# Merge gates of two branches projected earlier, inside the gated mixer and the attention mixer, and kept in HBM until their merges

## The chip, the cores and the metric

The kernel runs on one NeuronCore of a Trainium2 chip, as one launch. The metric is the device time of the launch in microseconds. Before the change it is 2548.67 us, the median of three runs that lie between 2547.56 and 2550.62 us. The profile is that of one further execution.

The engines are named as in the profile: PE (TensorE, the matrix engine), DVE (VectorE), ACT (ScalarE), POOL (GpSimd) and SP (SyncE, which here only issues DMAs). PEld is PE's loading of stationary operands.

## What is computed

Two layers of a hybrid backbone work on 640 tokens (512 latent tokens of one request, 128 context tokens of another) with a model width of 1024. Within a layer one input projection feeds three parallel mixers and three merge gates. The part that matters here, cut from the reference:

```python
(a_q, a_k, a_v, a_g, b_q, b_k, b_v, b_r, c_q, c_k, c_v,
 m_a, m_b, m_c) = jnp.split(h @ P['w_in'][l], points, axis=-1)
...  # y_a: retention of A; y_b: gated linear attention of B; y_c: differential attention of C
wb = P['w_branch'][l]
merged = (jax.nn.sigmoid(m_a) * (y_a.astype(dt) @ wb[0])
          + jax.nn.sigmoid(m_b) * (y_b.astype(dt) @ wb[1])
          + jax.nn.sigmoid(m_c) * (y_c.astype(dt) @ wb[2]))
out = merged @ P['w_out'][l]
```

The gates m_a, m_b and m_c, each 1024 wide, depend on the layer's input h alone, not on the mixers. The mixers' outputs are 512 wide. After the output projection follow a residual with LayerNorm, a gated MLP with a short convolution, and a second LayerNorm.

## The kernel before, in words

Activations lie transposed: a tile is 128 channels by 640 tokens, a "row" of SBUF. There are 59 rows (L486, L499), given out and taken back as tiles live and die; the last seven free ones are given only in program order. The layer's input h is 16 rows: eight tiles of 128 channels, each split into a high and a low fp32r part (hh, hl). Weights are split in the same way, and every product is made of three matmuls: high by high, low by high and high by low.

Weights come as blocks of 128 x 1024 in one fixed order, BLOCKS (L123). For each block a DMA on SP's queue loads w, ACT copies it to whi, and DVE or POOL forms wlo (`weights`, L731). Each of the three stages has three buffers, used strictly in that order. `take` (L756) fetches the next block and asserts that it is the one wanted, so the order of the blocks and the order of the program are one. `take` also paces the modulation: after every second block taken, the dot products of one further column of the modulation map are put into the program (`ada`, L686: two loads, four dot products on DVE). Blocks in the set QUIET (L124), which holds all blocks ahead of mixer A's, do not count for this pace.

`project` (L877) makes 128 output channels for all tokens: 48 matmuls into one of two PSUM tiles of the pool behind `slot`. A second pool of two, `mslot`, serves mostly the inner products of the mixers. A merge product (`gemm` into pbr) is 24 matmuls, since the mixers' outputs are 512 wide; one weight block holds two of them.

The order of the work is not that of the text. All operations are put into a list (`Program.add`, L225), and a planner (`place`, L291) builds a static order for every engine with modelled costs: for each engine in turn it takes the ready operation that stands first in the program, if its tile can have a buffer. Operations are offered up to 120 us of PE work ahead of where PE is, loads up to 40 us (L133). The hardware then runs these fixed orders, each engine and SP's queue in order, held by semaphores.

A layer runs in this order of the program:

- `mix_b` (L1003), the gated mixer, for two head pairs t = 0, 1: projections q, k, v and gate r; then a loop of nine levels (chunk lengths m = 1 to 256, counted by `lev`), each of which makes decayed queries and keys (eq, ek), a few small matmuls (psl, psp) and masked copies into st and stp; then the product with the values (po) and a normalization.
- `mix_a` (L1192), the retention mixer.
- `mix_c` (L1280), the attention mixer, as a generator with one step per head, with the merges of the second and the first branch put between its steps: four merges of branch 1 (mixer B) after heads 0 and 1, four of branch 0 (mixer A) after heads 2 and 3.
- the merges of branch 2 (mixer C), then the output projection (pout), the first LayerNorm, the MLP (pfa, pfb, pdn) and the second LayerNorm.

One merge is a pass of the loop in `branch` (L1437): it projects the gate's 128 channels (pmm, of block M_A, M_B or M_C), takes the tanh on ACT into a row g, makes the product pbr of the mixer's output with the branch's weights, multiplies on DVE ((g + 1) * pbr, in place), and adds to merged[j] on POOL, unless it is the first branch to be merged.

Of the kernel before, what the change touches and what calls it, by code (L numbers as in the profile page):

```python
# [10 lines left out]
F32 = mybir.dt.float32  # L11
F32R = mybir.dt.float32r
I32 = mybir.dt.int32
AF = mybir.ActivationFunctionType
# [59 lines left out]
def _blocks():  # L74
    b = []
    for t in range(2):
        b += [("in", B_Q + 128 * t), ("in", B_K + 128 * t)]
        b += [("v", B_V + 256 * t, i) for i in range(2)] if t else [("vg", i) for i in range(3)]
        b += [("in", B_R + 256 * t), ("in", B_R + 256 * t + 128)]
    for t in range(2):  # L80
        b += [("in", A_Q + 128 * t), ("in", A_K + 128 * t), ("v", A_V + 256 * t, 0), ("v", A_V + 256 * t, 1),
              ("in", A_G + 256 * t), ("in", A_G + 256 * t + 128)]
    for h in range(4):
        if h % 2 == 0:
            b += [("v", C_V + 128 * h, 0), ("v", C_V + 128 * h, 1)]
        b += [("in", C_Q + 128 * h), ("in", C_K + 128 * h)]
    return b
# [15 lines left out]
def _blocks_branch(x, m):  # L103
    b = []
    for j in range(8):
        b.append(("in", m + 128 * j))
        if j % 2 == 0:
            b.append(("br", x, j))
    return b


def _order():

    a = _blocks()
    c0 = a.index(("v", C_V, 0))
    o, c = a[:c0], a[c0:]
    fb, fa = _blocks_branch(1, M_B), _blocks_branch(0, M_A)
    o += c[0:4]
    o += c[4:6] + fb[0:6] + c[6:10] + fb[6:12] + c[10:12] + fa[0:6] + fa[6:12]
    return o + _blocks_branch(2, M_C) + _blocks_tail()  # L120


BLOCKS = _order()  # L123
# [360 lines left out]
def hybrid_kernel(ctx, tc, io):  # L484
# [392 lines left out]
    def project(ws, hs, name, *want, pool=slot):  # L877
        w = take(ws, *want)
        ps = pool(name)
        gemm(ps, w, 0, 8, hs)  # L880
        return ps
# [118 lines left out]
        return r[:, 0:512].rearrange("p (h x) -> p h x", h=4)  # L1000


    def mix_b(l, ws, hs, ys, save):  # L1003
        def mask(i, n=4):
            m, o = (m0, 128 * i) if i < 5 else (m1, 128 * (i - 5))
# [28 lines left out]
        for t in range(2):  # L1034
# [61 lines left out]
            while m < TL:  # L1096
                n = T if m < 128 else TL

                def v(x):
                    return x[:, 0:n].rearrange("p (b u m) -> p b u m", u=2, m=m)  # L1100

                eq = row("eq")
                act(v(eq)[:, :, 1, :], v(F)[:, :, 1, :], AF.Exp, scale=0.0625)
                act(v(eq)[:, :, 0, :], v(R)[:, :, 0, :], AF.Exp, scale=0.0625)
                tt(eq[:, 0:n], eq[:, 0:n], q[:, 0:n], MUL)
                if m == 1:
                    ek = k
                else:
                    ek = row("ek")
                    act(v(ek)[:, :, 0, :], v(G)[:, :, 0, :], AF.Exp, scale=0.0625)  # L1110
                    act(v(ek)[:, :, 1, :], v(H)[:, :, 1, :], AF.Exp, scale=0.0625)
                    tt(ek[:, 0:n], ek[:, 0:n], k[:, 0:n], MUL)
                bc = [128, n // (2 * m), m]
                tt(v(G)[:, :, 0, :], v(G)[:, :, 0, :], v(F)[:, :, 1, m - 1:m].to_broadcast(bc), ADD, POOL)
                tt(v(H)[:, :, 1, :], v(H)[:, :, 1, :], v(R)[:, :, 0, 0:1].to_broadcast(bc), ADD, POOL)
                tt(v(F)[:, :, 1, :], v(F)[:, :, 1, :], v(F)[:, :, 0, m - 1:m].to_broadcast(bc), ADD, POOL)
                tt(v(R)[:, :, 0, :], v(R)[:, :, 0, :], v(R)[:, :, 1, 0:1].to_broadcast(bc), ADD, POOL)
                if m < 256:
                    ps = mslot("psl")
                    for s in range(4):  # L1120
                        c = slice(128 * s, 128 * s + 128)
                        d = c if m < 128 else slice(128 * (s ^ 1), 128 * (s ^ 1) + 128)
                        mm_pair(*((bank(ps, h)[:, c], ek[a, c], eq[a, d]) for h, a in enumerate(rows)))
                    for h in range(2):
                        if m < 128:
                            copy_pred(out=chunks(st[h][:, 0:TL]), mask=mask(lev).bitcast(I32), data=chunks(bank(ps, h)))
                        else:
                            act(p128[h][:, 0:TL], bank(ps, h))
                else:
                    kk = [row("kk", F32R) for _ in range(2)]  # L1130
                    stack(kk, slice(0, TL), ek[:, 0:TL])
                    qq, ql = twice(eq, "q", TL)
                    for i in range(2):
                        ps = mslot("psl")
                        d = slice(256 * (1 - i), 256 * (1 - i) + 256)
                        for j in range(2):
                            c = slice(128 * (2 * i + j), 128 * (2 * i + j) + 128)
                            out = [bank(ps, h)[:, 256 * j:256 * j + 256] for h in range(2)]
                            mm_pair(*((out[h], kk[h][:, c], qq[h][:, d]) for h in range(2)), stop=False)
                            mm_pair(*((out[h], kk[h][a, c], ql[a, d]) for h, a in enumerate(rows)), start=False)  # L1140
                        for h in range(2):
                            act(p256[h][i][:, 0:512], bank(ps, h))
                if m < 128:
                    held.append((ek, eq, lev))
                    if len(held) == 2:
                        prompts()
                if m == 64:
                    for e, x in ((0, G), (1, H)):
                        kd = row("kd")
                        act(kd[:, 0:128], x[:, TL:T], AF.Exp, scale=0.0625)  # L1150
                        tt(kd[:, 0:128], kd[:, 0:128], k[:, TL:T], MUL)
                        states(kd[:, 0:128], vs, io["sgla"][l, e, t])
                lev += 1
                m *= 2
            qd = []
# [273 lines left out]
    for l in range(L):  # L1429
# [7 lines left out]
        def branch(x, mo, y):  # L1437
            yy = []
            for k in range(4):
                yh, yl = row("yh", F32R), row("yl", F32R)  # L1440
                split(yh, yl, y[k])
                yy.append((yh, yl))
            wb = None
            for j in range(8):
                ps = project(ws, hs, "pmm", "in", mo + 128 * j)
                g = row("g")
                act(g, ps[:, P0:P0 + T], AF.Tanh, scale=0.5)
                if j % 2 == 0:
                    wb = take(ws, "br", x, j)
                pb = slot("pbr")  # L1450
                gemm(pb, wb, 512 * (j % 2), 4, yy)
                stt(g, g, 1.0, pb[:, P0:P0 + T], ADD, MUL)
                if len(merged) < 8:
                    merged.append(g)
                else:
                    tt(merged[j], merged[j], g, ADD, POOL)
                yield
# [269 lines left out]
```

## Time and profile before

| | |
|---|---|
| median of three runs | 2548.67 us (2547.56 to 2550.62) |
| profiled execution | 2548.93 us |
| its span, from the first to the last instruction | 2547.2 us |
| mean granted PE clock | 0.985 |
| PE busy | 2467.7 us, 97% |
| DVE busy | 1619.7 us, 64% |
| ACT busy | 1117.3 us, 44% |
| POOL busy | 514.5 us, 20% |
| DMA, mean over the span | 95 GB/s, 242.87 MB |

A row of the table of stretches holds a stretch of the span in us, its length, and the busy time of each engine within it; "PEclk" is the share of full speed that PE's clock was granted. In a group or a timeline row, "out<-in" are the names that the program gave the tiles, L is the line of a helper, and what follows "<-" behind an idle time is what ended it. Nearly all matmuls are issued by two helpers (L533, L542), so they are told apart by the tile that they write: pmm are merge gates, pbr merge products, psl and psp the level products of the gated mixer, pvv value projections, psc scores of attention.

In this execution layer 0's gated mixer ends near 225 us, its attention mixer runs from about 342 to 640, its third branch to 731, and its output projection to 795. In layer 1 the gated mixer's level loops lie in 1352 to 1478, the attention mixer in 1597 to 1896, and the third branch ends at 1986.

### The profile page before, as it was taken

What the parts mean: (1) busy time and instruction counts of PE and PEld (TensorE: products, weight loads), DVE (VectorE), ACT (ScalarE), POOL (GpSimd) and SP (SyncE); (2) the same over time, 40 slices, a digit from 0 to 9 for tenths busy, and PEclk for the clock granted to TensorE, in tenths of its full rate; (3) what the DMA queues carried; (4) which work ended last, traced back from release to release, by engine and by line L of the source; (5) the groups of instructions that cost most, each with busy time, mean ns of one, the idle gap of its engine ahead of it and who ended that gap; (6) DMA issues with size and microseconds to landing.
All of it is one profiled execution on the core that took longest, in us unless ns stands there. A gap on an engine that the chain in (4) does not pass through costs nothing.

```text
span 2547.2 us, 41288 instructions
## 1 busy us (share of the span) xinstructions
PE 2467.7 (97%) x16762; PEld 2349.6 (92%) x16762; DVE 1619.7 (64%) x2898; ACT 1117.3 (44%) x1813; POOL 514.5 (20%) x391
## 2 busy tenths in 40 slices
PE   7999999999999999999989899999999999999997
PEld 4888889999998999999978789999999989999997
DVE  5788886566678865656868877744553564334346
ACT  3687654444325322223457676543442253122234
POOL 0452220121232600000346501100211132000001
PEclk9999999999999999999989899999999999999999
DMA  7122222322442333333422132112113222222222
GB/s 272 59 94 90 88 71 92 107 82 97 150 151 92 132 108 116 103 122 122 137 92 69 57 106 71 61 52 76 60 59 116 93 79 77 75 76 67 84 69 93
DMA packets 90335, 242.87 MB, mean 95 GB/s; under 512 B 10145, under 2 KB 16673, under 8 KB 90017
## 3 DMA queue, kind: packets, MB, share of 16 engines
q1 hardware_dynamic: 90144, 240.23, 28.5%
q8 instruction: 132, 2.16, 0.4%
q14 instruction: 59, 0.48, 0.1%
HBM read 232.85 MB, written 7.34 MB: 94 GB/s over the span
## 4 chain that ended last, share of the span: by engine, by line
PE 87%; DVE 6%; ACT 4%; DMA 2%; issue 1%; POOL 0%; SPq 0%; ACTq 0%; DVEq 0%; POOLq 0%
PE pmm L533 13%; PE pfb L533 12%; PE pfa L533 12%; PE pdn L533 12%; PE pbr L533 7%; PE pvv L533 6%; PE pout L533 4%; PE pcq L533 2%; PE pck L533 2%; PE pag L533 2%; PE psc L542 2%; PE ptc L533 1%; PE pr L533 1%; PE po L533 1%; PE psl L542 1%; DVE hf L580 1%
## 5 line engine op out<-in xcount | busy, mean ns | idle before, releaser
L554 ACT ACTIVATE whi<-w 128x1024 fp32r<-128x1024 f32 (+1 forms) x318 | 331.1, 1041 | 853.0 <-PE pdn L533 217.2
L566 DVE TENSOR_TENSOR wlo<-w,whi 128x1024 fp32r<-128x1024 f32 (+2 forms) x273 | 346.0, 1269 | 336.3 <-ACT whi L554 328.9
L566 POOL TENSOR_TENSOR wlo<-w,whi 128x1024 fp32r<-128x1024 f32 (+2 forms) x45 | 107.2, 2384 | 1221.9 <-ACT whi L554 1034.2
L533 PE MATMUL pmm<-hh,wlo 128*128 128x384 f32 (+1 forms) x768 | 239.2, 311 | 0.0
L533 PE MATMUL pmm<-hl,whi 128*128 128x384 f32 (+1 forms) x768 | 239.1, 311 | 0.0
L533 PE MATMUL pmm<-hh,whi 128*128 128x384 f32 (+1 forms) x768 | 238.7, 311 | 0.0
L533 PE MATMUL pfa<-hl,whi 128*128 128x384 f32 (+1 forms) x704 | 218.8, 312 | 4.5 <-DVE hl L580 4.3
L533 PE MATMUL pfa<-hh,whi 128*128 128x384 f32 (+1 forms) x704 | 218.8, 311 | 3.4 <-ACT hh L554 2.8
L533 PE MATMUL pfb<-hl,whi 128*128 128x384 f32 (+1 forms) x704 | 218.6, 311 | 0.0
L533 PE MATMUL pfb<-hh,whi 128*128 128x384 f32 (+1 forms) x704 | 218.5, 310 | 0.0
L533 PE MATMUL pdn<-fh,whi 128*128 128x384 f32 (+1 forms) x704 | 218.1, 310 | 0.0
L533 PE MATMUL pfb<-hh,wlo 128*128 128x256 f32 (+1 forms) x704 | 218.1, 310 | 0.0
L533 PE MATMUL pfa<-hh,wlo 128*128 128x384 f32 (+1 forms) x704 | 217.9, 310 | 0.0
L533 PE MATMUL pdn<-fl,whi 128*128 128x384 f32 (+1 forms) x704 | 217.9, 310 | 0.0
L533 PE MATMUL pdn<-fh,wlo 128*128 128x384 f32 (+1 forms) x704 | 217.7, 309 | 0.0
L533 PEld LDWEIGHTS pmm<-hh,whi 128*128 128x128 f32 x768 | 144.5, 188 | 1.0 <-issue 0.6
L533 PEld LDWEIGHTS pmm<-hl,whi 128*128 128x128 f32 x768 | 144.4, 188 | 0.9 <-issue 0.8
L533 PEld LDWEIGHTS pmm<-hh,wlo 128*128 128x128 f32 x768 | 144.5, 188 | 0.7 <-issue 0.5
L533 PE MATMUL pvv<-whi,hh 128*128 128x256 f32 (+1 forms) x480 | 138.7, 289 | 2.1 <-ACT q L554 1.0
L533 PE MATMUL pvv<-wlo,hh 128*128 128x256 f32 (+1 forms) x480 | 136.4, 286 | 3.8 <-DVE wlo L566 3.0
L533 PEld LDWEIGHTS pfa<-hl,whi 128*128 128x128 f32 x704 | 132.5, 188 | 7.5 <-DVE hl L580 7.4
L533 PE MATMUL pvv<-whi,hl 128*128 128x256 f32 (+1 forms) x480 | 137.5, 287 | 0.7 <-ACT z L554 0.7
(393 smaller groups left out, 6834.3 us busy)
## 6 DMA issues: line engine op xcount, KB each, us to landing
w<-W SPq DMA_DIRECT2D x270, 512.0 KB, 3.5
wada<-adaT SPq DMA_DIRECT2D x160, 256.0 KB, 3.8
w<-W SPq DMA_DIRECT2D x42, 448.0 KB, 3.2
wada<-adaW SPq DMA_DIRECT2D x32, 256.0 KB, 5.4
x<-xT SPq DMA_DIRECT2D x8, 320.0 KB, 6.1
dist<-rc SPq DMA_DIRECT2D x8, 320.0 KB, 3.6
xa<-xT SPq DMA_DIRECT2D x8, 320.0 KB, 6.3
xsave<-xa SPq DMA_DIRECT2D x8, 320.0 KB, 5.1
```

Of the source, the lines that this page charges most:

```text
L533: prog.add(("PE",), lambda e: nc.tensor.matmul(real(out), real(lhsT), real(rhs), start=start, stop=stop), [out], [lhsT, rhs], {"PE": c})
L542: nc.tensor.matmul(real(o), real(w), real(r), start=start, stop=stop)
L554: prog.add(("ACT",), lambda e: nc.scalar.activation(out=real(out), in_=real(in_), func=func, **{k: real(x) for k, x in kw.items()}), [out] ...
L566: prog.add(eng, lambda e: ENG[e].tensor_tensor(out=real(out), in0=real(a), in1=real(b), op=op), [out], [a, b], vcost(out.n), late=late, po ...
L580: prog.add(eng, lambda e: ENG[e].scalar_tensor_tensor(out=real(out), in0=real(a), scalar=real(s), in1=real(b), op0=op0, op1=op1), [out], [ ...
```

## The change

The gates of branch 1 (M_B) are no longer projected in its merges but in the gated mixer: a new helper `early` projects the 128 channels, takes the tanh into a row and stores the row to a tensor of its own in HBM. It is called behind the levels with an odd `lev` (1, 3, 5, 7), so four gates fall to each head pair. The gates of branch 2 (M_C) are projected by the same helper inside the passes of branch 1, that is, between the heads of the attention mixer, where M_B stood. In a pass of `branch` whose gate was kept, the row g is loaded from HBM and neither projection nor tanh is made. Branch 0 is as before. The order of the weight blocks follows. As the M_B blocks now stand ahead of mixer A's, they belong to QUIET and do not count for the pace of the modulation columns.

```diff
@@ _blocks
         b += [("in", B_R + 256 * t), ("in", B_R + 256 * t + 128)]
+        b += [("in", M_B + 128 * j) for j in range(4 * t, 4 * t + 4)]
@@ _blocks_branch
     for j in range(8):
-        b.append(("in", m + 128 * j))
+        if m is not None:
+            b.append(("in", m + 128 * j))
         if j % 2 == 0:
             b.append(("br", x, j))
@@ _order
-    fb, fa = _blocks_branch(1, M_B), _blocks_branch(0, M_A)
+    fb, fa = _blocks_branch(1, M_C), _blocks_branch(0, M_A)
     o += c[0:4]
     o += c[4:6] + fb[0:6] + c[6:10] + fb[6:12] + c[10:12] + fa[0:6] + fa[6:12]
-    return o + _blocks_branch(2, M_C) + _blocks_tail()
+    return o + _blocks_branch(2, None) + _blocks_tail()
@@ hybrid_kernel
+    def early(l, ws, hs, x, j):
+
+        ps = project(ws, hs, "pmm", "in", (M_A, M_B, M_C)[x] + 128 * j)
+        g = row("g")
+        act(g, ps[:, P0:P0 + T], AF.Tanh, scale=0.5)
+        name = f"gate{l}{x}{j}"
+        kept[l, x, j] = V(Tile_(None, [128, T], F32, name, dram.tile([128, T], F32, name=name)))
+        dma(kept[l, x, j], g, load=False)
+
+    kept = {}
+
@@ mix_b, in the level loop
+                if lev % 2:
+                    early(l, ws, hs, 1, 4 * t + lev // 2)
                 lev += 1
                 m *= 2
@@ branch
             for j in range(8):
-                ps = project(ws, hs, "pmm", "in", mo + 128 * j)
+                if x == 1:
+                    early(l, ws, hs, 2, j)
                 g = row("g")
-                act(g, ps[:, P0:P0 + T], AF.Tanh, scale=0.5)
+                if (l, x, j) in kept:
+                    dma(g, kept[l, x, j])
+                else:
+                    ps = project(ws, hs, "pmm", "in", mo + 128 * j)
+                    act(g, ps[:, P0:P0 + T], AF.Tanh, scale=0.5)
```

## The prediction

> **What bounds the kernel now.** I read the shares of the engines first, then the chain that ended last.
>
> ```profile
> PE 2467.7 (97%) x16762; PEld 2349.6 (92%) x16762; DVE 1619.7 (64%) x2898; ACT 1117.3 (44%) x1813; POOL 514.5 (20%) x391
> ...
> PE 87%; DVE 6%; ACT 4%; DMA 2%; issue 1%; POOL 0%; SPq 0%; ACTq 0%; DVEq 0%; POOLq 0%
> ```
>
> TensorE is busy for 97% of the span and carries 87% of the chain. The edit neither adds nor removes a matmul, so it can gain only where PE is idle or runs at a lower clock, and lose only where it opens a new gap. The second view is a table of stretches, cut at the stages (columns: stretch, length, busy time of PE, its weight loads, DVE, ACT, POOL, then clock, DMA share, GB/s). The gated mixer's level loops lie in 96:130 and 171:225 (layer 0, head pair 0 and 1) and in 1352:1395 and 1428:1478 (layer 1). 342:640 is layer 0's attention mixer with the merges woven in, 640:731 its third branch, 731:795 its output projection, and 1896:1986 is layer 1's third branch.
>
> ```profile
> 96.00:130.00 34.00, 30.34 (x283) 27.31 (x282) 31.12 (x39) 19.05 (x36) 24.26 (x25) 1.00 0.05 17
> 130.00:171.00 41.00, 40.56 (x289) 36.80 (x288) 32.33 (x37) 34.84 (x66) 19.92 (x19) 1.00 0.36 120
> 171.00:225.00 54.00, 48.07 (x363) 41.03 (x362) 48.17 (x74) 33.92 (x73) 26.21 (x26) 0.91 0.17 52
> ...
> 1352.00:1395.00 43.00, 40.80 (x367) 37.22 (x364) 35.06 (x46) 31.51 (x63) 26.18 (x30) 1.00 0.09 29
> ...
> 1428.00:1478.00 50.00, 39.47 (x297) 33.44 (x296) 45.19 (x72) 28.73 (x61) 22.60 (x24) 0.76 0.18 52
> ...
> 342.00:640.00 298.00, 295.06 (x2022) 280.81 (x2021) 203.30 (x398) 141.71 (x248) 51.87 (x32) 1.00 0.28 92
> 640.00:731.00 91.00, 91.00 (x623) 91.00 (x623) 60.75 (x120) 24.93 (x30) 31.76 (x16) 1.00 0.41 139
> 731.00:795.00 64.00, 62.69 (x413) 61.10 (x412) 53.83 (x103) 24.86 (x36) 20.23 (x10) 1.00 0.45 148
> ...
> 1896.00:1986.00 90.00, 90.00 (x619) 90.00 (x618) 29.27 (x31) 24.43 (x30) 16.70 (x8) 1.00 0.29 100
> ```
>
> PE idles 54.00 - 48.07 = 5.93 us and 50.00 - 39.47 = 10.53 us in the level loops of head pair 1, and 3.66 and 2.20 us in those of head pair 0. The first difference is that head pair 0 had the projections of head pair 1 to fill in, and head pair 1 little. In those two loops DVE is at 89% and 90%: their chain of level steps is DVE's. The third branch, from which PE work is taken, has no idle time at all. The timeline of PE and four stretches at the halved clock show the rest:
>
> ```profile
> 1437.22 3.08 PE L542 MATMUL psl<-eq,ek 64*128 64x128 f32 x32 [2.99 <-DVE st L601]
> ...
> 1442.47 2.08 PE L542 MATMUL psl<-eq,ek 64*128 64x128 f32 x16
> ...
> 1446.07 1.16 PE L542 MATMUL psl<-eq,ek 64*128 64x128 f32 x16 [0.81 <-DVE st L601]
> ```
>
> ```profile
> 202.41:212.65 10.24, 9.73 (x50) 8.83 (x47) 10.03 (x13) 8.04 (x18) 6.01 (x6) 0.50 0.36 117
> ...
> 1438.00:1444.90 6.90, 5.95 (x54) 5.41 (x52) 6.67 (x10) 3.85 (x10) 6.90 (x8) 0.51 0.14 38
> 1444.90:1448.30 3.40, 1.52 (x22) 1.17 (x20) 3.37 (x6) 1.11 (x3) 3.40 (x6) 1.00 0.27 82
> 1448.30:1465.30 17.00, 12.88 (x78) 11.01 (x79) 15.22 (x27) 6.96 (x16) 3.60 (x4) 0.50 0.07 14
> ```
>
> At the halved clock sixteen psl matmuls take 2.08 us instead of 1.16: 0.92 of 2.08, or 44% of the time, is lost.
>
> **The change part by part.** *Gates of the second branch into the level loops.* A projection is 48 matmuls, a merge product 24:
>
> ```profile
> 1901.64 7.08 PE pmm L533 x48
> ...
> 1929.80 3.55 PE pbr L533 x24
> ...
> L554 ACT ACTIVATE g<-pmm x48: 682/687/707, 388.7 to 1983.6; 128x640 f32<-128x640 f32 x48
> ```
>
> Each head pair gets four gates, 4 x 7.08 = 28.3 us of PE work that depends on nothing but weights. The PE's own level work leaves 10.5 us idle at most per loop, so the filler is enough. It stands after an odd level in program order and ahead of the next one; the planner takes the lowest ready operation, single matmuls at a time, so the gate goes first and the level step waits a few us, while PE stays busy. What stays idle is what the plan misjudged; I take for head pair 1 the idle time that its neighbour with filler has: 3.66 in layer 0, 2.20 in layer 1. Gain 5.93 - 3.66 = 2.3 and 10.53 - 2.20 = 8.3, together **10.6 us**. Bounds: 0 (the gates run after the loops) and all four, 22.3 us.
>
> *The clock.* With PE busy the halving goes. Busy time in the halved stretches is 9.73 + 5.95 + 12.88 = 28.6 us, of which 44% is saved: **12.6 us**; bounds 0 and half, 14.3. The row 1444.90:1448.30, PE busy 1.52 of 3.40 us and halved right behind it, says that a thin stretch is enough to lower the clock; 130:171, full, kept 1.00. [...]
>
> *What moves with them.* Eight weight blocks per layer (load, ACT, DVE or POOL split) and eight tanh (0.687 us each) move into the gated mixer: DVE gets 8 x 1.31 = 10.5 us more there, per layer. That lies under 8 x 7.08 = 56.6 us of new PE work, so DVE's share falls; without that cover it would cost its 10.5 us. The weights in layer 0's and 1's gated mixer drive no modulation columns (they are in QUIET), so four columns of layer 0 come later, in stages with DVE at 64% on the mean: nothing.
>
> *Gates of the third branch into the attention mixer.* In 342:640 the second branch's merges keep their PE work: 7.08 us of the third's gate in place of 7.08 us of their own. Nothing is gained, PE has 2.9 us idle there. At its end the third branch used to give 56.6 us more PE work per layer; is that cover missed? In layer 1:
>
> ```profile
> 1896.17 0.83 DVE L566 TENSOR_TENSOR yl<-rstd,yh 128x640 fp32r<-128x640 f32 x1 [0.81 <-ACT yh L554]
> ```
>
> The last attention output is split at 1897.0, and PE works on products of the first branch until the third's first gate begins at 1901.64. The third's own product, which now stands there, is ready 4.6 us before. So the cover is enough, with that margin; the loss is bounded by 0 and, if the last head came 10 us later, 5.4 us. I take **1 us** for layer 1, near to the row.
>
> *Gate tiles through HBM.* Per layer 16 stores and 16 loads of 320 KB. The nearest rows are the residual's, stored and loaded again, beside a weight block's:
>
> ```profile
> w<-W SPq DMA_DIRECT2D x270, 512.0 KB, 3.5
> ...
> xsave<-xa SPq DMA_DIRECT2D x8, 320.0 KB, 5.1
> xa<-xsave SPq DMA_DIRECT2D x8, 320.0 KB, 6.1
> ```
>
> A load lands 6.1 us after issue, and its store (5.1 us) was issued a stage earlier, so only the row of SBUF can hold it back. Loads may be issued 40 us of PE work ahead, and the 16 rows of the input's split halves come free after the first branch's last gate, which is earlier than before. Taken as nothing; bound: the first load has to wait for those rows, 6.1 us less the 3.5 us of the first product, 2.6 us per layer, within the 5.4 above. A store waits on SP's queue for its tanh, and the next weight loads stand behind it; see the rivals.
>
> *The third branch, now short.* It becomes 8 x 3.55 = 28.4 us instead of 85.0. In layer 1 DVE's 29.27 us (less eight weight splits, 10.5) fit. In layer 0 the modulation columns and the scaling of the residual run there too. Here are the costliest groups of DVE, then of POOL, in 640:795:
>
> ```profile
> L566 DVE TENSOR_TENSOR wlo<-w,whi 128x1024 fp32r<-128x1024 f32 x22 | 28.8, 1312 | 14.1 <-ACT whi L554 13.6
> L586 DVE SCALAR_TENSOR_TENSOR wada<-wada,sB 128x512 f32<-128x512 f32 x27 | 21.7, 813 | 0.2
> L586 DVE SCALAR_TENSOR_TENSOR junk<-wada,sB 128x512 f32<-128x512 f32 x27 | 20.1, 755 | 3.1 <-DMA wada<-adaT 3.1
> ...
> L566 DVE TENSOR_TENSOR ml<-g,mh 128x640 fp32r<-128x640 f32 x8 | 6.6, 825 | 9.5 <-ACT mh L554 9.5
> ...
> L566 DVE TENSOR_TENSOR acc<-acc,xa 128x384 f32<-128x384 f32 (+1 forms) x8 | 4.5, 561 | 0.2
> ...
> L580 DVE SCALAR_TENSOR_TENSOR hf<-xa,ms,rs 128x256 f32<-128x256 f32 (+1 forms) x4 | 3.5, 940 | 1.2 <-ACT rs L554 1.2
> ...
> L566 DVE TENSOR_TENSOR xa<-xa,mu 128x256 f32<-128x256 f32 x8 | 3.2, 471 | 0.3 <-ACT mu L554 0.3
> ```
>
> ```profile
> L566 POOL TENSOR_TENSOR g<-g 128x640 f32<-128x640 f32 x9 | 18.6, 2070 | 60.9 <-DVE g L580 60.9
> L572 POOL TENSOR_SCALAR xa<-xa 128x640 f32<-128x640 f32 x8 | 15.9, 2002 | 1.3 <-DMA xa<-xT 1.3
> L566 POOL TENSOR_TENSOR wlo<-w,whi 128x1024 fp32r<-128x1024 f32 x4 | 10.1, 2514 | 39.3 <-ACT whi L554 39.3
> L566 POOL TENSOR_TENSOR sq<-sq 128x384 f32<-128x384 f32 x5 | 7.7, 1534 | 2.8 <-DVE sq L566 2.6
> ```
>
> The stretch of 155 us becomes 155 - 56.6 = 98.4 us. DVE's 60.75 + 53.83 = 114.6 us lose eight splits (10.5) and four columns: 27 pairs of dot products are 13.5 columns at (21.7 + 20.1) / 13.5 = 3.1 us, so 12.4. There stay 91.7 us, 93% of the stretch. It fits, but in the first 28 us a merge may wait for a column's dot products. On PE that costs between 0 and, when DVE and POOL can't overlap, 19.4 us (rival 1). I take **5 us**: nearer to 0, since DVE alone still fits.
>
> *Sum:* -10.6 - 12.6 + 1 + 5 = -17.2 us. The profiled execution took 2548.93 us, of which its span is 2547.2; it is 0.26 us above the median of 2548.67, so on the median **2531.5 us**.
>
> **The rivals.** *1: VectorE and GpSimd take turns in layer 0's third branch.* All the DVE groups shown take their data from SBUF: 28.8 + 21.7 + 20.1 + 6.6 + 4.5 + 3.5 + 3.2 = 88.4 us, and POOL's 52.3. Less the 10.5 and the 12.4 there are 117.8 us for 98.4, 19.4 too many. With that in the place of 5 the time is 2548.67 - 10.6 - 12.6 + 1 + 19.4 = 2545.9, too near to no change to be told from it. For it: the adds g<-g take 2.07 us on the mean in layer 0 here, after 1.56 at the least elsewhere:
>
> ```profile
> L566 POOL TENSOR_TENSOR g<-g x32: 1555/1688/2651, 554.2 to 1987.3; 128x640 f32<-128x640 f32 x32
> ```
>
> Against it: columns may run 40 us ahead, where DVE is at 68%. [...]
>
> *2: the gates do not fill.* If the two PSUM slots that the gates need are held by other tiles through the level loops, the gates run behind them. The first two terms are 0 and the losses stay: 2548.67 + 6 = 2554.7. For it: in 1428:1478 projections of the next mixer stood ready and PE idled. Against it: a gate's slot is freed by one tanh of 0.687 us, not by a queue of DVE work.
>
> *3, slower: SP's queue.* SP issues in order, and each of the 32 stores waits for its tanh; weight loads behind it are late.
>
> ```profile
> SPq L618 <- ACT kt L554: 119.1, 16, 35.9
> ...
> PE pvv L533 <- DVE wlo L566: 3.0, 2, 2.0
> ...
> L554 ACT ACTIVATE whi<-w 128x1024 fp32r<-128x1024 f32 (+1 forms) x318 | 331.1, 1041 | 853.0 <-PE pdn L533 217.2
> ```
>
> For it: the 16 small stores of states made SP wait 119.1 us, 35.9 at once. Against it: PE waited for split weights 3.0 us in all, since three blocks stand ready, 21 us of PE work. It decides once a store is waited for longer than that. A block then costs 3.5 (landing) + 1.04 (ACT) + 1.31 (DVE) = 5.8 us of idle PE; at one store in four, 8 x 5.8 = 46 us, and the time is 2531.5 + 46 = 2578.
>
> *4: everything is recovered:* 22.3 + 14.3 us and no loss, 2512.
>
> **How the numbers follow.** The forecast has 0.62, its own range 2520 to 2544. Rival 1 at its full price has 0.14, rival 2 0.07, rival 3 0.09, rival 4 0.08. A measurement of this kernel can tell 0.2%, 5.1 us, from no change. Faster: 0.62 + 0.08 = 0.70; same: rival 1, 0.14; slower: 0.07 + 0.09 = 0.16. The range 2515 to 2549 reaches from the greater part of rival 4 to rival 1 and leaves out rivals 2 and 3.
>
> **What would show it.** Right: gate projections (pmm) between the psl of all four level loops; the halved clock gone around 202 to 213 and 1438 to 1465; PE idle of head pair 1's loops down to about that of head pair 0; the third branch some 28 us long in both layers and the attention mixers as long as before. Wrong: PE idle beside pbr or pout behind DVE or POOL in layer 0 (rival 1), pmm grouped behind the loops (rival 2), PE waiting for weight splits in the mixers with SP behind a gate's tanh (rival 3). The forecast falls if the level loops lose less than 10 us of idle and halved time together.

## The result and the profile after

The changed kernel takes 2524.65 us (median; 2523.45 to 2525.73), beside 2548.11 us for the kernel before on the same chip: a ratio of 0.9908, with a 95% interval of 0.9891 to 0.9925. That is 24.0 us less than the median before the prediction, and 23.5 less than the runs beside it; 17.2 were forecast. The shares of the engines on the page of the changed kernel:

```profile
PE 2458.0 (97%) x16762; PEld 2338.9 (93%) x16762; DVE 1613.0 (64%) x2898; ACT 1114.4 (44%) x1813; POOL 513.5 (20%) x387
```

The matmuls are the same 16762. PE's busy time fell by 9.7 us all the same, since a matmul at the halved clock is busy for longer (2.08 against 1.16 us for sixteen psl in the kernel before). The level loops of the changed kernel, in the table of stretches (stretch, length, busy time of PE, PEld, DVE, ACT, POOL, then granted clock, DMA share, GB/s; layer 0 with head pairs 0 and 1, then layer 1):

```profile
98.00:133.00 35.00, 32.75 (x283) 29.73 (x282) 32.17 (x42) 15.06 (x34) 27.95 (x27) 1.00 0.26 89
...
196.00:246.00 50.00, 48.26 (x401) 43.75 (x398) 41.03 (x69) 31.16 (x66) 20.62 (x22) 1.00 0.40 139
1341.00:1390.00 49.00, 48.77 (x406) 44.18 (x405) 39.98 (x55) 27.76 (x60) 30.20 (x30) 1.00 0.24 84
...
1438.00:1488.00 50.00, 48.69 (x413) 43.98 (x410) 41.09 (x67) 31.40 (x65) 20.22 (x23) 1.00 0.40 134
```

The clock is whole in all four. PE idles 1.74 us in head pair 1 of layer 0 and 1.31 us in that of layer 1, where it had idled 5.93 and 10.53 us. The longest gap left in the level loops is 1.33 us, at 103.06. In the timeline of PE the gates (pmm) stand between the level products (psl), here in layer 1:

```profile
1453.02 1.16 PE L544 MATMUL psl<-eq,ek 64*128 64x128 f32 x16 [0.20 <-ACT eq L556]
1454.12 0.45 PE L535 MATMUL pmm<-hl,whi 128*128 128x384 f32 x1
...
1459.60 1.16 PE L544 MATMUL psl<-eq,ek 64*128 64x128 f32 x16
```

To account for all of the time I cut both traces at the same events of PE (first psl, first psc, last pnc, last pbr, last pout). Of the kernel before, these stretches are layer 0's gated and retention mixers, its attention mixer, its third branch, its output projection, the way from there to layer 1's first level, and layer 1's mixers:

```profile
97.20:357.70 260.50, 249.16 (x1811) 224.28 (x1810) 219.58 (x337) 181.14 (x332) 96.45 (x87) 0.98 0.25 81
357.70:637.20 279.50, 277.30 (x1907) 263.54 (x1907) 188.74 (x376) 125.79 (x225) 43.59 (x28) 1.00 0.28 91
637.20:731.70 94.50, 94.50 (x645) 94.50 (x645) 63.77 (x127) 27.77 (x34) 33.32 (x17) 1.00 0.41 140
731.70:794.10 62.40, 61.80 (x407) 60.40 (x406) 52.71 (x102) 24.75 (x36) 19.33 (x10) 1.00 0.45 151
794.10:1345.80 551.70, 538.22 (x3568) 527.03 (x3566) 374.95 (x741) 192.34 (x265) 110.55 (x83) 0.98 0.34 114
1345.80:1612.70 266.90, 251.93 (x1823) 228.93 (x1822) 214.87 (x329) 180.67 (x332) 91.23 (x85) 0.96 0.23 74
```

And of the changed kernel the same:

```profile
98.10:402.90 304.80, 299.14 (x2195) 275.83 (x2194) 220.09 (x342) 193.44 (x348) 101.03 (x88) 1.00 0.28 93
402.90:682.00 279.10, 276.90 (x1907) 263.13 (x1907) 192.31 (x385) 126.23 (x226) 36.93 (x22) 1.00 0.34 117
682.00:720.70 38.70, 38.34 (x260) 37.77 (x258) 37.69 (x57) 13.77 (x17) 16.32 (x8) 1.00 0.56 189
720.70:790.20 69.50, 64.24 (x411) 61.11 (x410) 61.60 (x122) 25.99 (x38) 26.06 (x13) 1.00 0.43 145
790.20:1341.50 551.30, 538.38 (x3565) 528.43 (x3565) 379.11 (x750) 191.82 (x265) 111.30 (x81) 0.98 0.34 112
1341.50:1645.70 304.20, 301.03 (x2207) 277.48 (x2206) 219.16 (x343) 192.91 (x348) 99.51 (x89) 1.00 0.28 93
```

Eight gates are 8 x 7.08 = 56.6 us of PE work. The two mixers that took them up grew by 304.80 - 260.50 = 44.3 us in layer 0 and by 304.20 - 266.90 = 37.3 us in layer 1. So they give 12.3 and 19.3 us, 31.6 together: 17.5 us less idle time (11.34 to 5.66 and 14.97 to 3.17), and, by difference, 14.1 us of busy time from matmuls that no longer run at the halved clock. The third branch shrank by 55.8 us in layer 0, 0.8 less than its work did. Layer 0's output projection lost 69.50 - 62.40 = 7.1 us: DVE is busy for 61.60 of 69.50 us there, and for 37.69 of 38.70 ahead of it. All other stretches agree within 1 us. The spans give 2547.2 - 2524.0 = 23.2 us.

On DVE's side of the third branch (682.00 to 720.70), the groups of dot products in the changed kernel (count, then busy time and mean ns) are

```profile
L588 DVE SCALAR_TENSOR_TENSOR junk<-wada,sB 128x512 f32<-128x512 f32 x8 | 9.4, 1194 | 0.0
...
L588 DVE SCALAR_TENSOR_TENSOR wada<-wada,sB 128x512 f32<-128x512 f32 x8 | 6.8, 856 | 0.0
```

What PE waits for in the output projection, in the timeline of the changed kernel, is the low parts of the merged sum, and these wait for DVE:

```profile
725.10 0.44 PE L535 MATMUL pout<-ml,whi 128*128 128x384 f32 x1 [0.69 <-DVE ml L568]
728.86 0.45 PE L535 MATMUL pout<-ml,whi 128*128 128x384 f32 x1 [1.56 <-DVE ml L568]
```

### The profile page after: what moved, and what is told of

Read it like the earlier page. It is cut to its first block, busy times and chain, and to the rows that moved or that the text cites. A ratio compares the mean times of both kernels' runs of the same rounds, so it can differ in the third digit from the quotient of the medians.

```text
span 2524.0 us, 41456 instructions
## 1 busy us (share of the span) xinstructions
PE 2458.0 (97%) x16762; PEld 2338.9 (93%) x16762; DVE 1613.0 (64%) x2898; ACT 1114.4 (44%) x1813; POOL 513.5 (20%) x387
## 4 chain that ended last, share of the span: by engine, by line
PE 89%; DVE 6%; ACT 3%; issue 1%; DMA 1%; SPq 0%; ACTq 0%
PE pmm L535 13%; PE pfb L535 12%; PE pfa L535 12%; PE pdn L535 12%; PE pvv L535 7%; PE pbr L535 6%; PE pout L535 4%; PE pcq L535 2%; PE pck L535 2%; PE pag L535 2%; PE psc L544 2%; PE pr L535 2%; PE ptc L535 1%; PE psl L544 1%; PE paq L535 1%; PE po L535 1%
## 5 line engine op out<-in xcount | busy, mean ns | idle before, releaser
L568 DVE TENSOR_TENSOR wlo<-w,whi 128x1024 fp32r<-128x1024 f32 (+1 forms) x276 | 355.4, 1288 | 327.1 <-ACT whi L556 310.7
L568 POOL TENSOR_TENSOR wlo<-w,whi 128x1024 fp32r<-128x1024 f32 (+2 forms) x42 | 98.8, 2353 | 1192.8 <-ACT whi L556 991.2
```

The lines of the kernel that those rows point to most:

```text
L568: prog.add(eng, lambda e: ENG[e].tensor_tensor(out=real(out), in0=real(a), in1=real(b), op=op), [out], [a, b], vcost(out.n), late=late, po ...
```

## The experiments

Each is an edit of the changed kernel, and each time is given with the ratio to the kernel before, run on the same chip. Stretches are cut at the same events of PE as above, in one profiled execution each. The planner builds new orders for every edited kernel, so an edit can also shift work that it does not name.

### One part alone

```diff
@@ e1_second_only: the third branch projects its own gates
-                if x == 1:
-                    early(l, ws, hs, 2, j)
@@ e2_third_only: the second branch projects its own gates
-                if lev % 2:
-                    early(l, ws, hs, 1, 4 * t + lev // 2)
```

(The order of the weight blocks follows in both.)

> Only the second branch's gates move (into the level loops); the third branch projects its own gates as before. If the gain comes from the level loops and the loss from the shortened third branch of layer 0, this keeps the gain of the loops (some 11 us in layer 0, 19 in layer 1) and has no loss at layer 0's output projection: 2517 to 2522 us, with the third branch back at about 94 us in both layers and PE idle below 1 us at layer 0's output projection. Rival: the third branch's gates are needed as cover between the heads of attention; then PE idles 8 to 15 us per layer in the attention mixer and the time is 2533 to 2550 us.

Measured: 2550.31 us, ratio 1.0011 (1.0002 to 1.0021). The expectation fell and its rival held in kind, with more idle time in layer 0 than its 8 to 15 us and less in layer 1. In this kernel the stretches of layer 0's gated and retention mixers, of its attention mixer and of its output projection, and then of layer 1's attention mixer:

```profile
97.50:402.20 304.70, 299.02 (x2195) 275.69 (x2194) 222.50 (x345) 191.85 (x345) 99.76 (x86) 1.00 0.29 96
402.20:646.10 243.90, 227.03 (x1524) 209.93 (x1524) 170.90 (x332) 116.29 (x214) 40.95 (x24) 0.98 0.25 83
...
740.40:802.90 62.50, 61.89 (x407) 60.50 (x405) 52.64 (x102) 24.75 (x36) 19.34 (x10) 1.00 0.45 151
...
1659.30:1888.30 229.00, 222.01 (x1521) 207.03 (x1521) 144.54 (x250) 114.13 (x212) 46.08 (x25) 1.00 0.19 63
```

The loops gain just what they gain in the changed kernel (304.70), and the output projection loses nothing (62.50). But the attention mixer, which gave up 56.6 us of PE work, should have shrunk from 279.5 to 222.9 us and took 243.9, with PE idle for 16.9 us; layer 1's took 229.0 where 222.3 were due, with 7.0 us idle. The longest of these waits in layer 0 is for ACT's step of the softmax (pc), which reads the score tiles in PSUM:

```profile
496.29 1.57 PE L544 MATMUL psc<-qkp 64*128 64x128 f32 x4 [2.83 <-ACT pc L556]
```

So the gates of the second branch had been filler in attention, and moving them out costs there 21.0 and 6.7 us, most of what the loops gain.

> Only the third branch's gates move (into the second branch's merges, between the heads); the second branch's gates stay in its merges. If this part gains nothing and costs what layer 0's output projection lost in the changed kernel, the time is 2553 to 2558 us, PE idle 4 to 6 us at layer 0's output projection and none in layer 1's. Rival: this part is neutral and the loss came with the other part: 2546 to 2550 us.

Measured: 2557.32 us, ratio 1.0039 (1.0026 to 1.0052), as expected. Layer 0's gated and retention mixers and its output projection in this kernel:

```profile
97.10:354.90 257.80, 246.60 (x1813) 221.48 (x1812) 217.25 (x335) 181.13 (x331) 95.23 (x85) 0.99 0.25 82
...
729.80:799.20 69.40, 64.17 (x411) 61.05 (x410) 61.45 (x122) 25.89 (x38) 26.07 (x13) 1.00 0.42 145
```

Layer 0's mixers with the level loops keep their idle time: 11.2 us here, 11.3 before. The 2.7 us by which they are shorter are busy time (clock 0.99 for 0.98). The output projection has its 69.4 us. Alone, one part costs some 3 us and the other some 10; together they gain 23 to 24. The first part takes filler out of the attention mixer, the second puts as much back, and only its price in layer 0 is left.

### Where the gates stand in the loops, and how many

```diff
@@ e5_behind_loop
-                if lev % 2:
-                    early(l, ws, hs, 1, 4 * t + lev // 2)
                 lev += 1
                 m *= 2
+            for i in range(4):
+                early(l, ws, hs, 1, 4 * t + i)
@@ e6_pair1_only: gates 0 to 3 stay in the second branch's merges
-                if lev % 2:
+                if lev % 2 and t:
```

> The four gates of a head pair are called behind its level loop instead of after the odd levels, so that they stand behind the levels in program order. If all that counts is that work is ready for PE within the planner's reach, the planner puts them between the levels all the same and the time stays at 2521 to 2528 us. Rival: it counts that a gate stands ahead of the next level; then a part of the idle time and of the halved clock of head pair 1 returns and the time is 2530 to 2540 us.

Measured: 2523.70 us, ratio 0.9906 (0.9891 to 0.9921), the changed kernel's time. The two stretches of mixers take 304.5 and 303.8 us (304.8 and 304.2 in the changed kernel). Yet the planner did not put all gates between the levels: in head pair 1's loops, in both layers, 79 of their 192 matmuls stand between level products and 113 behind the last psl, ahead of po. So either place serves; a part of the gates is filler enough.

> Only the four gates of head pair 1 are made early; those of head pair 0 stay in the merges. If the gain is the idle time and the halved clock of head pair 1's loops, which one loop's filler covers, nearly all of it stays: 2522 to 2528 us, with no halved clock in the gated mixers. Rival: each gate made early gains by itself, so half the gates give half of it: 2534 to 2539 us.

Measured: 2541.47 us, ratio 0.9974 (0.9962 to 0.9985). Neither expectation was right: the gain is 0.26%, less than a third of the changed kernel's, and in layer 1's mixers a little of the halved clock is left (0.99). Layer 0's and layer 1's gated and retention mixers, and layer 0's output projection:

```profile
97.00:377.50 280.50, 272.60 (x2004) 248.45 (x2002) 218.62 (x342) 187.05 (x338) 92.47 (x83) 1.00 0.27 88
1344.70:1627.10 282.40, 273.94 (x2013) 250.74 (x2012) 221.30 (x351) 187.33 (x339) 88.48 (x82) 0.99 0.26 84
724.20:793.70 69.50, 64.31 (x410) 61.20 (x410) 61.45 (x122) 25.85 (x38) 26.07 (x13) 1.00 0.42 145
```

They grew by 20.0 and 15.5 us for 28.3 us of gates, so half of the gates gives 8.3 + 12.8 = 21.1 us in the loops, two thirds of the 31.6. The price in layer 0's output projection is paid in full (69.5). The rest of the shortfall stands in layer 1's attention mixer, 312.9 us long with 5.1 us of idle PE, where 278.9 + 28.3 = 307.2 were due; what holds it there stays open.

### Layer 0's output projection

Three edits aim at DVE's load there, one at the length of the third branch. The changed kernel was run beside the first three of them:

> The changed kernel once more, beside the variants of it, as their measure: 2522 to 2527 us, PE idle of about 5 us in layer 0's output projection.

Measured: 2525.29 us (2523.02 to 2526.49), ratio 0.9911 (0.9898 to 0.9925), its output projection 69.4 us.

```diff
@@ e3_columns_early, take(): columns of layer 0 faster, none in its third branch and output projection
-        turn[0] += blk not in QUIET
+        if at[0] == 0 and (blk[0] == "out" or blk[0:2] == ("br", 2)):
+            step = 0
+        elif at[0] == 0 and blk[0] not in ("up", "dn"):
+            step = 4
+        else:
+            step = 3
+        turn[0] += step * (blk not in QUIET)
@@ e3_columns_early, the pace
-GAP = 2
+GAP = 6
@@ e4_scale_on_act
-                ts(xa, xa, ALPHA, MUL, eng=POOL)
+                act(xa, xa, scale=ALPHA)
@@ e9_half_third: the even gates are projected in the third branch
-                if x == 1:
+                if x == 1 and j % 2:
```

> The changed kernel with layer 0's modulation columns paced faster in the mixers (four columns for six blocks instead of three), so that none fall into its third branch and output projection; the same columns are computed. If the dot products on VectorE are what layer 0's output projection lost its time to, that stage goes from 69.5 to 63 to 65 us and the time falls by 4 to 6 us against the changed kernel: 2518 to 2521 us. Rival: it is the rest of VectorE's and GpSimd's work, crowded into a third of the time; then the stage stays at 68 to 70 us and the time within 2 us of the changed kernel's.

Measured: 2549.20 us, ratio 1.0002 (0.9993 to 1.0011). The stage did what was expected, and the whole did not. The attention mixer and the output projection of layer 0:

```profile
402.80:711.90 309.10, 291.72 (x1903) 274.03 (x1903) 201.86 (x430) 125.88 (x224) 38.77 (x23) 0.93 0.34 114
...
750.60:814.70 64.10, 62.83 (x410) 60.83 (x409) 46.91 (x86) 25.34 (x36) 18.13 (x9) 1.00 0.39 132
```

The output projection came back to 64.1 us, so most of its loss (5.4 of 7.1 us) came with the dot products. But with more of them in the mixers, layer 0's attention is 30.0 us longer, with 17.4 us of idle PE and a clock of 0.93, though DVE is busy for 201.86 of 309.10 us only. PE stalls in two places, from 500 to 519 and from 604 to 614, and in the first DVE is idle too and waits for PE's scores:

```profile
516.07 0.72 DVE L593 TENSOR_REDUCE mx<-psc 128x1 f32<-128x128 f32 x2 [7.12 <-PE psc L544]
```

In the second, dot products do stand among the softmax's steps (609.75 to 612.44). So in the larger stall it is neither DVE's share nor a dot product ahead of the softmax. PE's order holds nothing but the steps of the softmax between 500 and 519, while in the kernel with the columns late (below) the next head's projections stand at that place. Why the planner's order changed so was not found.

> The changed kernel with layer 0's residual scaled by ALPHA on ScalarE instead of GpSimd (eight tiles, 2.0 us each on GpSimd). If VectorE and GpSimd take turns at SBUF, VectorE's operations behind 726 us no longer stretch (wlo, dot products and sq from 1.2 to 2.5 us back to their shortest) and the time falls by 2 to 4 us: 2520 to 2523 us. Rival: they do not hinder one another and the time stays within 1 us of the changed kernel's.

Measured: 2525.36 us, ratio 0.9914 (0.9899 to 0.9929): no change against the kernel beside it. The stage is shorter by 3 us. In the profiled execution 1.6 us of it are lost again up to layer 1's first level and 0.9 in layer 1's output projection; which step took them was not settled.

```profile
720.40:786.60 66.20, 63.26 (x407) 60.46 (x407) 57.77 (x124) 25.30 (x37) 20.54 (x11) 1.00 0.40 136
```

> The changed kernel with only the odd four of the third branch's gates made in the attention mixer; the even four are projected in the third branch, between the short merges. If attention needs some 17 us of filler in layer 0 and 7 in layer 1 (what PE idled when it had none of these gates) and layer 0's third branch suffers from being short, 28 us of filler are enough and the 28 us left relieve VectorE: output projection of layer 0 at 63 to 65 us, attention without new idle time, 2517 to 2521 us. Rival: four gates do not reach the places where attention idles; then PE idles 5 to 10 us there and the time is 2524 to 2532 us.

Measured: 2537.58 us, ratio 0.9963 (0.9950 to 0.9975): the rival, and worse. The attention mixer and the output projection of layer 0:

```profile
402.80:671.20 268.40, 256.14 (x1715) 239.29 (x1715) 181.44 (x356) 120.20 (x218) 41.59 (x25) 0.97 0.28 97
...
737.30:800.40 63.10, 61.82 (x407) 60.30 (x405) 51.59 (x108) 25.49 (x37) 21.29 (x12) 1.00 0.42 142
```

The output projection is well (63.1), but attention idles 12.3 us, though 28.3 us of filler were given for a measured need of 17. From 480 to 505, where most of this idle time lies, PE's order holds no gate, no merge product and no projection of the next head. Filler counts where it stands, not by its sum.

The last edit of this group takes the dot products the other way, behind the output projection:

```diff
@@ e12_columns_late, take()
-        turn[0] += blk not in QUIET
+        turn[0] += blk not in QUIET and not (at[0] == 0 and (blk[0] == "out" or blk[0:2] == ("br", 2)))
@@ the gate of the second residual, fetched before its first use
-        g2 = gate(l, 1)
...
+            if gi == 0:
+                g2 = gate(l, 1)
             if f0 < FT:
```

> The changed kernel with layer 0's modulation columns left out of its third branch and output projection and made in the MLP instead, eight of them before its first product with w_down, which is the first to need them; the same columns are computed. If layer 0's output projection lost its 5 to 7 us to these dot products, and the MLP has room for them (VectorE 68% busy there), that stage goes from 69.4 to about 64 us, the attention mixer stays at 279 us and the time is 2518 to 2521 us. Rival: the MLP's start needs VectorE as well; then the gain is given back there and the time is 2523 to 2528 us.

Measured: 2520.02 us (2519.59 to 2520.83), ratio 0.9889 (0.9872 to 0.9905), as expected, and faster than both kernels: 5 us under the changed kernel's 2525.29. The two were run on different chips, and the intervals of their ratios overlap by 0.0007, but no run of one kernel lies within the runs of the other. Layer 0's attention mixer, third branch and output projection, the way from there to layer 1's first level, and layer 1's attention mixer:

```profile
402.80:681.90 279.10, 276.90 (x1908) 263.11 (x1908) 191.90 (x386) 126.17 (x226) 39.65 (x23) 1.00 0.35 118
681.90:719.80 37.90, 37.90 (x260) 37.84 (x259) 22.45 (x20) 13.70 (x17) 27.95 (x16) 1.00 0.30 95
719.80:785.20 65.40, 63.02 (x410) 60.98 (x410) 48.43 (x87) 25.35 (x36) 19.54 (x9) 1.00 0.42 135
```

```profile
785.20:1334.60 549.40, 535.07 (x3566) 525.20 (x3565) 374.52 (x725) 192.12 (x267) 128.87 (x90) 0.99 0.34 113
1639.10:1918.70 279.60, 277.21 (x1906) 263.24 (x1906) 176.88 (x341) 125.08 (x225) 33.62 (x20) 1.00 0.32 109
```

DVE's load in the third branch fell from 37.69 to 22.45 us, PE is idle nowhere in it, and the output projection is 4.1 us shorter than in the changed kernel. The stretch with the MLP did not take up more of them: it has 136 dot products, where the changed kernel has 143, since the columns come in one queue and those left out push the later ones back. The load ended up in layer 1's attention mixer, with 43 dot products for 10 and DVE busy for 176.88 us for 155.64, and that mixer took 279.6 us for 279.1.

The same with the scaling on ACT:

> The same, with layer 0's residual scaled on ScalarE instead of GpSimd. If VectorE alone was the limit, no further gain: within 1 us of the kernel with the columns late. If the two engines' turns at SBUF still stretch VectorE's work, a further 1 to 3 us: 2516 to 2519 us.

Measured: 2519.55 us (2514.47 to 2520.71), ratio 0.9883 (0.9868 to 0.9898): no difference from the kernel with the columns late, though the output projection is down to 64.2 us.

### The dot products taken out of layer 0's attention

With the gates of the second branch moved alone, layer 0's attention idles 16.9 us and layer 1's 7.0. Layer 0's has 46 of the modulation's dot products on DVE, layer 1's 9, and e3_columns_early, where layer 0's grew, has 83. This edit stands on e1_second_only and cuts those dot products from 512 elements to 8:

```diff
@@ e14_second_only_short_dots, on top of e1_second_only
-    def ada(l, u):
+    def ada(l, u, n=512):
-                dot((junk if g == 0 else w)[:, 0:512], w[:, 0:512], ...
+                dot((junk if g == 0 else w)[:, 0:n], w[:, 0:n], ...
...
-            ada(*pending.pop(0))
+            att = at[0] == 0 and (blk[0] in ("in", "v") and C_Q <= blk[1] < M_C or blk[0] == "br" and blk[1] < 2)
+            ada(*pending.pop(0), 8 if att else 512)
```

> The kernel in which only the second branch's gates move (attention without the third's as filler), with the dot products of the modulation columns that are paced by layer 0's attention mixer cut to 8 of their 512 elements; loads and number of operations stay, so that part of the modulation is not computed. If these columns are why layer 0's attention idled 16.9 us there and layer 1's only 7.0, layer 0's attention mixer goes from 243.9 us to 229 to 233 and the time from 2550 to 2535 to 2540 us. Rival: the softmax chain alone makes PE idle; then the mixer stays at 240 to 244 us and the time at 2546 to 2551 us.

Measured: 2543.05 us (2539.46 to 2544.21), ratio 0.9975 (0.9965 to 0.9985), between the two expectations. The attention mixers of layer 0 and layer 1 in this kernel, and what PE waits for in the first:

```profile
402.30:642.60 240.30, 228.04 (x1522) 212.56 (x1522) 141.55 (x326) 114.05 (x212) 41.63 (x25) 0.96 0.26 84
...
1655.90:1885.40 229.50, 222.26 (x1521) 207.26 (x1521) 144.46 (x250) 114.21 (x212) 46.38 (x25) 1.00 0.19 63
```

```profile
PE psc L544 <- ACT pc L556: 3.3, 3, 1.9
PE ptc L549 <- ACT pc L556: 3.0, 1, 3.0
```

DVE's busy time in layer 0's attention fell from 170.90 to 141.55 us, below that of layer 1. PE's idle time fell with it, from 16.9 to 12.3 us, but layer 1's is 7.2, and the stage takes 240.3 us, where 229 to 233 were due if the dot products were the reason. So by the stage the rival holds: the dot products are 4.6 of some 10 us of extra idle time, and the waits for the softmax on ACT stay without them. Of the 10.8 us that layer 0's mixer still takes longer, 5.0 are idle and the rest is busy time at a lower clock (0.96, after 0.98 with the dot products whole). Another 2.6 us of the kernel's gain stand in layer 1's output projection, which the edit does not touch.

A step that sets the layers apart can be seen, though not what puts it there. A merge product needs one of the two PSUM tiles behind `slot`, and here it waits for qc, the step on DVE that reads the projection pcq and so frees one:

```profile
506.63 0.69 PE L535 MATMUL pbr<-yh,whi 128*128 128x384 f32 x1 [2.15 <-DVE qc L568]
```

This pcq was finished at 472.9 and pck at 484.9, but DVE's order has the steps that read them at 505.89 and 508.9. Until then both tiles were held, and PE could begin no merge product during the stalls. In e1_second_only the two waited 27.7 and 23.9 us in layer 0 and 15.9 and 15.0 in layer 1; in the changed kernel 0.9 and 6.3 at the same head. That the held tiles cause the stalls was not shown by an edit. Why DVE's order has these steps so late stays open; one candidate is the columns' loads, which stayed in this kernel.

### The way through HBM

```diff
@@ e7_twice
         dma(kept[l, x, j], g, load=False)
+        dma(twin, g, load=False)
...
+                    dma(g, kept[l, x, j, 1])
                     dma(g, kept[l, x, j])
```

> The changed kernel with each gate stored twice and loaded twice (32 more stores, 32 more loads of 320 KB). If the way through HBM is hidden, the time stays within 2 us of the changed kernel's: 2523 to 2527 us. Rival: stores hold up the weight loads on SP's queue; then each of the 32 further round trips costs 0.2 to 0.5 us and the time is 2531 to 2541 us.

Measured: 2526.83 us (2525.86 to 2527.46), ratio 0.9915 (0.9900 to 0.9930): 1.5 us above the changed kernel for 32 more round trips, with overlapping runs. In the total the way through HBM is all but hidden. It is not without effect on a stage: in the profiled execution layer 0's output projection took 73.4 us, 3.9 more than in the changed kernel, with 27 dot products in it for 21.

## Why the prediction was right, point by point

**Idle time of the loops: right in kind, too small.** Forecast was 10.6 us, measured 17.5. The term that was mis-sized is the idle time that stays: I gave head pair 1 what head pair 0 had idled before, 3.66 and 2.20 us. It kept 1.74 and 1.31, and head pair 0 itself, for which I had counted nothing, went from 3.66 to 2.25 us in layer 0 and from 2.20 to 0.23 in layer 1. The neighbour had not been full of filler. The experiment with head pair 1 alone agrees: a third of the gain belongs to head pair 0's gates.

**The clock: right.** 12.6 us forecast, some 14 measured by difference, within the bound of 14.3. The halved stretches around 202 and 1438 to 1465 are gone. That the term comes whole was my estimate. In the kernel before, the clock fell to 0.50 or 0.51 at 202.4, 1438.0 and 1448.3, behind three thin stretches: PE was busy for 1.42 of 3.40 us in 199.00:202.40, for 1.01 of 4.00 in 1434.00:1438.00 and for 1.52 of 3.40 in 1444.90:1448.30. In the changed kernel's loops the longest gap is 1.33 us, and the clock stayed at 1.00. Which gap or which busy share lowers it was not shown.

**The order in the loops: right, and of no matter.** The timeline shows a gate's matmuls between two psl; with the gates behind the loop in program order a part of them ends up there as well, and the time is the same. Rival 2 (the gates do not fill) is out.

**The attention mixer: right by a sum, not seen as a part of the gain.** I wrote that nothing is gained where a gate of the third branch takes the place of the second's. As a sum it held (279.5 and 279.1 us). But I looked for missing cover only at the mixer's end, not between its heads; without this half of the edit the whole gain is gone (ratio 1.0011). At the end no stall of weight came: PE idles 0.36 us in layer 0's third branch and not at all in layer 1's. But PSUM tiles held by other work, which I had feared for the level loops (rival 2), are seen in attention when the third's gates are left out; there I had not asked for them.

**Layer 0's third branch: right, 5 us forecast for 7.9** (7.1 in the output projection, 0.8 in the merges). It was DVE, as rival 1 had it, at less than its full price of 19.4 us; the columns are the cause of 4.1 to 5.4 of the 7.1 by the two experiments that move them. Layer 1 lost 0.3 us in its third branch instead of 1.

**HBM and SP's queue: nothing, as forecast.** In the changed kernel's waits of SP, and of PE for weights:

```profile
SPq L620 <- ACT g L556: 166.2, 21, 15.9
...
PE pvv L535 <- DVE wlo L568: 3.2, 2, 2.2
```

SP did wait 166.2 us for tanhs, 15.9 at the most, under the 21 us from which rival 3 would decide, and PE's wait for split weights went from 3.0 to 3.2 us.

The sum: 31.6 gained in the loops for 23.2 forecast, 8.2 lost in the third branches and layer 0's output projection for 6. Both sides were forecast too small, and as they have opposite signs, it is partly luck that the sum came as near as 17.2 for 24.0.

## What to carry to other kernels

Work without dependences is a resource to be placed: when it is moved into one stage's gaps, ask what it was filling where it stood, and put something else there. Two halves of such an edit, tried one at a time, can each look like a loss. And a stage that is cut to a third keeps the work of the other engines; here some 16 us of dot products (9.4 and 6.8 in the groups of DVE shown above) were a part of the limit, and paced later they cost nothing that can be seen, even though the queue of columns then put 33 more of them into layer 1's attention.

## What the runs showed that I had not expected

**VectorE and GpSimd took turns in layer 0's third branch.** DVE and POOL in the timeline of the changed kernel:

```profile
713.33 2.07 DVE L588 SCALAR_TENSOR_TENSOR wada<-wada,sB 128x512 f32<-128x512 f32 x1
...
717.94 2.19 DVE L568 TENSOR_TENSOR ml<-g,mh 128x640 fp32r<-128x640 f32 x1
```

```profile
712.82 2.03 POOL L568 TENSOR_TENSOR g<-g 128x640 f32<-128x640 f32 x1 [1.56 <-DVE g L582]
...
717.03 2.41 POOL L568 TENSOR_TENSOR g<-g 128x640 f32<-128x640 f32 x1 [2.17 <-DVE g L582]
```

A dot product takes 0.68 us here when nothing holds it up, a split ml 0.81:

```profile
712.60 0.81 DVE L568 TENSOR_TENSOR ml<-g,mh 128x640 fp32r<-128x640 f32 x1
...
720.91 0.68 DVE L588 SCALAR_TENSOR_TENSOR junk<-wada,sB 128x512 f32<-128x512 f32 x1
```

The dot product in the first fence begins at 713.33 during POOL's add and ends at 715.40, 0.55 us after the add's end at 714.85. The split ml begins at 717.94 and ends at 720.13, 0.69 us after POOL's at 719.44. The dot products at 682.07, 697.25, 705.91 and 721.52, which begin during such an add, end 0.55 or 0.56 us after it as well. The add at 712.82 in turn begins during the split of 712.60 and ends 1.44 us after it, where an add takes 1.56 us when nothing holds it up (at 1868.39). So in these pairs the later one stands still, but for some 0.12 us, until the other is done. Not every pair does so: in layer 1 the product of g and pbr on DVE that begins at 1963.11, during the add of 1961.75 to 1963.77, takes 0.82 us, and none of the 48 of its kind takes longer. Yet relieving POOL alone (scaling on ACT) did not change the time of the kernel (2525.36 us beside 2525.29).

**Layer 0's attention is fragile.** With the columns of e3_columns_early its attention is 30.0 us longer for 9.6 us more on DVE (201.86 against 192.31), while layer 1's in e12_columns_late took 21.2 us more on DVE for 0.5 us. With four of the eight gates it idles 12.3 us, while layer 1's attention in the same kernel (e9_half_third) takes 251.6 us, 2.6 of them idle:

```profile
1656.80:1908.40 251.60, 249.04 (x1713) 234.98 (x1713) 148.19 (x262) 119.35 (x217) 39.28 (x23) 1.00 0.23 76
```

I had taken the dot products for the whole reason. Cutting them short removes not half of the difference in idle time. What the long stalls have in common is PE's order: no gate, merge product or projection stands in them, and in some of them finished projections hold both PSUM tiles that such work needs. What makes the planner order layer 0 so stays open.
